# Expert rows by DRAM for two groups and by selection matmuls for two, with gate/up in interleaved halves

## The chip, the cores and the metric

The kernel runs on one core of one Trainium2 chip. The metric is the device time of one execution in microseconds; of several runs the median stands.

## The reference, cut to what matters

A backbone of two layers works on 512 latent tokens and, in the first layer, 256 context tokens, 1024 wide, in float32. Each layer has a mixer and then a hierarchical mixture of experts: a token picks one of four groups, then two of the group's eight experts.

```python
g_idx = jnp.argmax(g_logit, axis=-1)
top_v, top_i = lax.top_k(e_logit, TOP_K)
w = g_prob * jax.nn.softmax(top_v, axis=-1)
e_idx = g_idx[:, None] * EXPERTS_PER_GROUP + top_i
...
(jax.nn.silu(xblk @ w_gate[e]) * (xblk @ w_up[e])) @ w_down[e]
```

Each token's two results, times their weights, are added, gated per channel and added to the stream. An expert's weights are 1024 x 512 twice and 512 x 1024: 6 MiB, of which a layer has 32.

## The kernel before

The whole is one program: mixer 0 (phase_a), experts 0, mixer 1 (phase_c), experts 1 (moe, called once per layer, with 768 and 512 tokens). The stream is kept turned, channels on partitions, in eight tiles XT. Only the parts in moe are changed, and the banks in setup and ps.

Experts are taken in 16 pairs (pr_); the layout has pair r hold two experts of group r % 4. A pair has 128 slots, at most, and usually, 64 for each expert; spare slots of one may go to the other. gather (L1210) is an indirect load on POOL that brings a pair's 128 rows from DRAM (h2d) into xg; a slot with no token fetches row 0, which holds zeros. xpose (L1322) turns them with eight PE transposes. gate_up (L1345) runs 8 steps of two matmuls, the two halves of 64 columns of the array, on the 64 rows of one expert; ACT's silu and two DVE operations make h, turned (L1360) turns it, down (L1369) multiplies by the third weight, and place (L1379) adds both halves to y in SBUF.

When more than 64 rows fall to one expert of a pair, its second half is done in overflow (L1513), under tc.If; if the pair holds more than 128, what is left is gathered into xs and done in blocks of 64 in a second If (a spill). Every engine branches there. HINTED (L45) gives PE, DVE and ACT a hint of the branch ahead of it.

All pairs but the last are "direct": scatter (L1429) writes y to two rows per token in DRAM (yd) by an indirect store on POOL, slots with no token being out of bounds. The last pair's y is split into two float32r parts and added by selection matmuls (combine, L1387, and token_rstd, L1460). At the end fetch_rows (L1553) reads all of yd back by SP, DVE adds a token's two rows, and fetched (L1453) turns them in PE into the banks in which the selection of pair 15 is then accumulated; add_gated adds to XT, squares are summed for the next norm.

Weights come through a ring of eight tiles of 2 MiB, seven of a pool and one extra (spare), in a written order: per pair four gate/up halves, then two downs. load(k) (L971) issues the next k on SP. The tile that a load replaces is the one eight loads earlier, so SP waits for it to be read. What sets the order is the program: PE's order is pinned as written, DVE, ACT and POOL may be ordered within a stretch between two Ifs. Per pair:

```python
if pr_: load(1)
h = gate_up(W[0], ...); h = gate_up(W[1], ..., turn(0, h))
overflow(pr_, W, xts[pr_], y, ys, direct)
load(4)
pd = down(W[0], ht[0], turn(1, h)); load(1)
xts[pr_ + 1] = xpose(...); gather(pr_ + 2)
place(y, 0, pd); place(y, 1, down(W[1], ht[1]))
if direct: scatter(y, yrow[:, pr_:pr_ + 1])
```

PSUM is eight banks: seven in a pool for all uses (ps) and one (bank) that takes every eighth, or, in the expert loop, the gate/up of each pair's first expert.

## Time and profile before

| | |
|---|---|
| Median of 3 runs | 1804.42 us (1800.4 to 1805.56) |
| The profiled execution | 1808.97 us |
| Its span in the trace | 1807.2 us |
| Mean granted clock of TensorE, share of full | 0.944 |
| Busy: PE, PEld, DVE, ACT, POOL | 1533.7, 816.8, 706.2, 410.3, 283.9 us |
| Moved by DMA | 545.23 MB, 302 GB/s over the span |

Slices are 45.2 us. PE is TensorE's matmuls, PEld its weight loads beside them, SPq and POOLq the queues from which DMAs are issued. Busy PE counts waiting inside a pipeline, so 85% does not say that PE is the limit; which wait ends last has to be looked for in each stage. A tile named ring is a weight tile (or a piece of scratch that uses its slot), mk and hb are small tiles of the expert stage, ps and psg are banks.

### The profile page before, as it was taken

Reading aid. Unit: us, or ns where it says so; the run is one execution under the profiler, and the core shown is the slowest. Engines: PE = TensorE matmul, PEld = TensorE weight load, DVE = VectorE, ACT = ScalarE, POOL = GpSimd, SP = SyncE. Lnnn points to the kernel's source line nnn. Section 1 sums busy time; section 2 is a strip of 40 time slices with the busy share of each in tenths; the row PEclk is TensorE's granted clock in tenths of the full one; section 3 lists DMA queues with packets and bytes.
Section 4 is the critical chain, followed back from the end, with each engine's and each line's share of the span. In section 5 each row is a group of like instructions: output and inputs, shape, how many; then the busy total and the mean of one; then the engine's idle time right before and its main releaser. Section 6 shows DMA issues by size and latency. Waiting matters only on the chain. (4 is left out here: it accounts for less than half of the span.)

```text
span 1807.2 us, 21981 instructions
## 1 busy us (share of the span) xinstructions
PE 1533.7 (85%) x8285; PEld 816.8 (45%) x8285; DVE 706.2 (39%) x1342; ACT 410.3 (23%) x930; POOL 283.9 (16%) x232
## 2 busy tenths in 40 slices
PE   6997997988788779767898899996897888888776
PEld 4775686332222223223686878784222322223223
DVE  6799867211111101113636876554111211112115
ACT  4211632110100001001445554332110111011012
POOL 1231343001010101000232202022000101101001
PEclk9999998999989989998999999997899998999998
DMA  8997173799999968999221131488989999999991
GB/s 300 316 298 272 51 291 129 315 399 423 409 426 429 427 247 354 429 427 416 97 88 53 54 104 46 141 293 334 396 343 425 426 385 426 426 387 426 428 366 69
DMA packets 90052, 545.23 MB, mean 302 GB/s; under 512 B 10136, under 2 KB 32296, under 8 KB 63792
## 3 DMA queue, kind: packets, MB, share of 16 engines
q1 hardware_dynamic: 80240, 510.55, 70.7%
q0 software_dynamic: 9536, 31.50, 4.5%
q8 instruction: 112, 1.84, 0.4%
q14 instruction: 164, 1.34, 0.2%
HBM read 511.82 MB, written 34.09 MB: 302 GB/s over the span
## 5 line engine op out<-in xcount | busy, mean ns | idle before, releaser
L56 PE MATMUL ps<-ring,mk 128*64 128x512 f32 x1408 | 326.7, 607 | 35.3 <-DMA ring<-gu 27.2
L56 PE MATMUL ps<-ring,hb 128*64 128x512 f32 x1024 | 265.8, 654 | 100.4 <-DVEq L1517 67.0
L56 PE MATMUL psg<-ring,mk 128*64 128x512 f32 x1024 | 235.8, 610 | 24.2 <-DMA ring<-gu 24.2
L1383 DVE TENSOR_TENSOR mk<-ps,mk 64x512 f32<-64x512 f32 x128 | 88.2, 689 | 319.3 <-PE ps L56 299.5
L56 PEld LDWEIGHTS ps<-ring,mk 128*64 128x64 f32 x1408 | 98.1, 139 | 231.0 <-issue 178.8
L56 PEld LDWEIGHTS ps<-ring,hb 128*64 128x64 f32 x1024 | 72.0, 146 | 239.9 <-issue 160.7
L56 PEld LDWEIGHTS psg<-ring,mk 128*64 128x64 f32 x1024 | 77.6, 140 | 175.6 <-issue 173.0
L1357 DVE SCALAR_TENSOR_TENSOR hb<-mk,mk,ps 128x128 f32<-128x128 f32 x80 | 24.2, 345 | 307.5 <-ACT mk L1353 307.5
L510 DVE SCALAR_TENSOR_TENSOR cv<-u,convw,cv 128x798 f32<-128x798 f32 x120 | 139.1, 1215 | 3.5 <-ACT cv L508 3.0
L1357 DVE SCALAR_TENSOR_TENSOR hb<-mk,mk,psg 128x128 f32<-128x128 f32 x64 | 19.4, 345 | 220.5 <-ACT mk L1353 220.5
L1366 ACT ACTIVATE hb<-ps 128x128 f32<-128x128 f32 x128 | 28.9, 275 | 301.5 <-PE ps L56 301.5
L1211 POOL DMA_INDIRECT xg<-h2d,mk x30 | 30.9, 1029 | 391.3 <-PE ps L56 391.3
L1353 ACT ACTIVATE mk<-psg 128x256 f32<-128x256 f32 x32 | 12.3, 383 | 345.2 <-PE psg L56 188.6
L1567 POOL MEMSET mk<- 128x1024 f32 x32 | 30.5, 953 | 307.3 <-DMA yd<-mk,mk 301.2
L111 PE MATMUL ps<-hh,hi 128*128 128x512 f32 (+1 forms) x232 | 71.4, 365 | 7.2 <-ACT hh L285 7.2
L95 POOL TENSOR_TENSOR lo<-wc,hi 128x1024 fp32r<-128x1024 f32 (+3 forms) x25 | 44.0, 1764 | 175.4 <-ACT hi L89 127.4
L113 PE MATMUL ps<-hl,hi 128*128 128x512 f32 (+1 forms) x232 | 68.6, 349 | 0.0
L115 PE MATMUL ps<-hh,lo 128*128 128x512 f32 (+1 forms) x232 | 68.0, 347 | 0.0
L95 POOL TENSOR_TENSOR lo<-wo,hi 128x512 fp32r<-128x512 f32 x32 | 44.6, 1399 | 114.5 <-ACT hi L89 112.9
L1430 POOL DMA_INDIRECT yd<-mk,mk x30 | 30.2, 1007 | 183.5 <-DVE mk L1383 183.5
L111 PE MATMUL ps<-hi,hi 128*128 128x512 f32 (+1 forms) x191 | 57.1, 348 | 2.2 <-DVE ptl L691 2.0
L113 PE MATMUL ps<-lo,hi 128*128 128x512 f32 (+1 forms) x191 | 55.2, 336 | 3.4 <-POOL lo L95 3.4
(372 smaller groups left out, 2328.8 us busy)
## 6 DMA issues: line engine op xcount, KB each, us to landing
ring<-gu SPq DMA_DIRECT2D x125, 2048.0 KB, 24.0
ring<-dn SPq DMA_DIRECT2D x59, 2048.0 KB, 26.8
mw<-modw SPq DMA_DIRECT2D x72, 512.0 KB, 5.7
yd<-mk SPq DMA_DIRECT2D x20, 512.0 KB, 7.6
ring<-yd SPq DMA_DIRECT2D x10, 1024.0 KB, 12.7
mw<-modh SPq DMA_DIRECT2D x16, 512.0 KB, 7.4
ring<-dn SPq DMA_DIRECT2D x8, 1024.0 KB, 23.0
wi<-w_in SPq DMA_DIRECT2D x12, 512.0 KB, 7.8
```

The source lines that it names most:

```text
L56: i = f(*a, **k)
L95: nc.gpsimd.tensor_tensor(lo, src, hi, op=ALU.subtract)
L111: T.matmul(o, lh, rh, start=start, stop=False)
L113: T.matmul(o, lh, rl, start=False, stop=False)
L115: T.matmul(o, ll, rh, start=False, stop=stop)
L510: nc.vector.scalar_tensor_tensor(acc, u[:, j:j + LO], cw[:, j:j + 1], acc, op0=ALU.mult, op1=ALU.add)
L1211: return G.indirect_dma_start(out=xg, out_offset=None, in_=h2d, in_offset=bass.IndirectOffsetOnAxis(ap=idi[:, pr_:pr_ + 1], axis=0), bound ...
L1357: V.scalar_tensor_tensor(h[b], sg[:, cs_], wcol, po[:, 256 + P * b:384 + P * b], op0=ALU.mult, op1=ALU.mult)
L1366: S.activation(ht[b], po[:, :P], AF.Copy)
L1383: V.tensor_tensor(d, p, d, op=ALU.add)
L1430: G.indirect_dma_start(out=yd, out_offset=bass.IndirectOffsetOnAxis(ap=rows, axis=0), in_=y, in_offset=None, bounds_check=2 * n - 1, oob_i ...
L1567: G.memset(y, 0.0)
```

## The change

The pairs are taken in a new order (ORDER); p is the position, r_ the pair. Pairs of groups 0 and 1 (r_ % 4 < 2) are direct and scattered to yd. Pairs of groups 2 and 3 are split and kept, and combine adds them by selection matmuls during the next pair, in two halves; the last four positions are all of this kind, the last one's combine stands in token_rstd. The last direct pair is at position 11. From position 12 the extra ring tile is the stage: read_back fetches a tile of 128 tokens from yd by two indirect loads on POOL, zeros first, only rows of groups 0 and 1; merge adds a token's two rows, turns them in PE and adds them to XT, two tiles at each position from 13 on.

Gate/up is split: the second half of a pair's first expert runs at the start of its position (the first half in the position before), the second expert's in pieces, between which turning, combine, the first down, the If, and the next pair's transposes stand. The order of loads follows. Slots with no token are now out of bounds in the gather, which then leaves what was there. The hint of the branch is given for PE alone. Banks are six and two.

```diff
-HINTED = [mybir.EngineType.PE, mybir.EngineType.DVE, mybir.EngineType.Activation]
+ORDER = (0, 2, 1, 3, 4, 6, 5, 8, 7, 9, 12, 13, 10, 11, 14, 15)
...
-if self.whole and not hold and self.turn % 8 == 0:
+if self.whole and not hold and self.turn % 4 == 0:
...
-self.psum = E(tc.tile_pool(name="psum", bufs=7, space=PSUM))
-self.psg = E(tc.tile_pool(name="psg", bufs=1, space=PSUM))
+self.psum = E(tc.tile_pool(name="psum", bufs=6, space=PSUM))
+self.psg = E(tc.tile_pool(name="psg", bufs=2, space=PSUM))
...
-    lq, spare = [], []
+    lq, spare, taken = [], [], []
...
+        gu = lambda p, i, h: A["gu"][l, 2 * ORDER[p] + i, h]
+        dn = lambda p, i: A["dn"][l, 2 * ORDER[p] + i]
+        todo = [gu(0, 0, 0)]
+        for p in range(16):
+            todo += [gu(p, 0, 1), gu(p, 1, 0), dn(p, 0), gu(p, 1, 1), dn(p, 1)] + ([gu(p + 1, 0, 0)] if p < 15 else [])
+        for src in todo:
+            a = slot() if len(lq) % 8 != 6 or taken else spare[0].tile([P, 4096], F32, name=self.nm("ring"), tag="ring")
+            for c in ((slice(0, 2048), slice(2048, 4096)) if len(lq) >= 3 * NE - 3 else (slice(0, 4096),)):
+                pin(eng[0].dma_start(out=a[:, c], in_=src[:, c]))
+            lq.append(a)
+            yield
...
+    pad = sm(16)
+    V.tensor_scalar(pad, idf, 0.5, 8192.0, op0=ALU.is_lt, op1=ALU.mult)
+    V.tensor_tensor(idi, pad, idf, op=ALU.add)
...
+    back, bf = keep([2, nt], I32), [sm(nt), sm(nt)]
+    V.tensor_tensor(bf[0], og[:, :, 0], og[:, :, 1], op=ALU.add)
+    V.tensor_scalar(bf[0], bf[0], -8192.0, 8191.0, op0=ALU.mult, op1=ALU.add)
+    V.tensor_tensor(bf[1], self.cols[:, C_TOK:C_TOK + nt], self.cols[:, C_TKL:C_TKL + nt], op=ALU.add)
+    V.tensor_tensor(bf[0], bf[0], bf[1], op=ALU.add)
+    V.tensor_copy(back[:, 0], bf[0])
+    V.tensor_scalar(back[:, 1], bf[0], float(n), None, op0=ALU.add)
...
-    V.tensor_copy(nbf[:, 2:4, 16:32], nbf[:, 2:4, 0:16])
+    for p, r_ in enumerate(ORDER):
+        G.tensor_copy(nbf[:, 2:4, 16 + p:17 + p], nbf[:, 2:4, r_:r_ + 1])
...
+    def weights(p):
+        return [(lambda h, i=i: lq[6 * p + 2 * i + h * (1 + i)].rearrange("p (k c f) -> p k c f", k=4, c=2),
+                 lambda i=i: lq[6 * p + 3 + 2 * i].rearrange("p (k d) -> p k d", k=4)) for i in range(2)]
...
+    def gate_up(po, W, xt, s, ks):
+        for k in ks:
...
+                T.matmul(po[64 * c:64 * c + 64, :], xt[:, k, s], W[0](k // 4)[:, k % 4, c, :], start=k == 0, stop=k == KD - 1)
+    def gated(po, wcol):
+        h = hb[:, 0]
+        S.activation(h.rearrange("p b c -> p (b c)"), po[:, :256], AF.Silu)
...
+    def extra(W, xt, s, wcol):
+        po = self.ps()
+        gate_up(po, W, xt, s, range(KD))
+        return down(W, turned(gated(po, wcol)))
...
-        yh, yl, sel = pend
-        ahead = fetched(0)
...
+            combine([m], *pend)
...
+    def overflow(pos_, pr_, Ws, xt, y, ys, direct):
         shared[0] = {}
-        if pr_ % 8 == 0:
-            spills[:] = nc.values_load_multi_w_load_instructions(nbi[0:1, 2, pr_:pr_ + 8])[1]
-        with tc.If(spills[pr_ % 8] > 0, label=f"ov{l}_{pr_}"):
-            tc.mark_branch_hint_location(f"sp{l}_{pr_}", "LikelyTaken", HINTED)
+        if pos_ % 8 == 0:
+            spills[:] = nc.values_load_multi_w_load_instructions(nbi[0:1, 2, 16 + pos_:24 + pos_])[1]
+        with tc.If(spills[pos_ % 8] > 0, label=f"ov{l}_{pr_}"):
+            tc.mark_branch_hint_location(f"sp{l}_{pr_}", "LikelyTaken", [mybir.EngineType.PE])
...
+    def read_back(t_):
+        v = stage[0][:, 2048 * (t_ % 2):2048 * (t_ % 2) + 2048].rearrange("p (q c) -> p q c", q=2)
+        for q in range(2):
+            G.memset(v[:, q], 0.0)
+            G.indirect_dma_start(
+                out=v[:, q], out_offset=None, in_=yd,
+                in_offset=bass.IndirectOffsetOnAxis(ap=back[:, q, t_:t_ + 1], axis=0),
+                bounds_check=2 * n - 1, oob_is_err=False)
+    def merge(t_):
+        v = stage[0][:, 2048 * (t_ % 2):2048 * (t_ % 2) + 2048].rearrange("p (q c) -> p q c", q=2)
+        V.tensor_tensor(v[:, 0], v[:, 0], v[:, 1], op=ALU.add)
+        for hh in range(2):
+            po = self.ps()
+            for q in range(4):
+                T.transpose(po[:, P * q:P * q + P], v[:, 0, P * (4 * hh + q):P * (4 * hh + q) + P], self.ident)
+            for q in range(4):
+                k = 4 * hh + q
+                x = self.XT[k][:, P * t_:P * t_ + P]
+                V.scalar_tensor_tensor(x, po[:, P * q:P * q + P], gate[:, k, vt(t_):vt(t_) + 1], x, op0=ALU.mult, op1=ALU.add)
+        if t_ + 2 < nt:
+            read_back(t_ + 2)
+    mc = lambda m: slice(P * m, P * m + P)
+    xt = xpose(xg, slice(0, P), "xt", 2)
+    gather(ORDER[1])
     load(1)
...
+    pend, stage = None, []
+    pa = self.bank()
+    gate_up(pa, weights(0)[0], xt, half(0), range(4))
+    slot_weights()
+    for p, r_ in enumerate(ORDER):
+        direct = r_ % 4 < 2
+        y = keep([D], tag="y3", bufs=3)
+        ys = [xs] if direct else [keep([D], F32R, tag="y3", bufs=3) for _ in range(2)]
+        G.memset(y[64:128], 0.0)
+        W = weights(p)
+        tc.mark_branch_hint_location(f"ov{l}_{r_}", "LikelyTaken", [mybir.EngineType.PE])
+        if p == 12:
+            stage.append(spare[0].tile([P, 4096], F32, name=self.nm("ring"), tag="ring"))
+            for t_ in range(2):
+                read_back(t_)
+        gate_up(pa, W[0], xt, half(0), range(4, KD))
+        h = gated(pa, wd[:, 0, 2 * r_:2 * r_ + 1])
+        if p > 12 and 2 * (p - 13) < nt:
+            merge(2 * (p - 13))
+        other = self.bank()
+        gate_up(other, W[1], xt, half(1), range(2))
+        ht = turned(h)
+        if p == 0:
+            spill_table()
+        if pend:
+            combine(range(4), *pend)
+        gate_up(other, W[1], xt, half(1), range(2, 4))
+        if pend:
+            combine(range(4, KD), *pend)
+        place(y, 0, down(W[0], ht), False)
+        overflow(p, r_, W, xt, y, ys, direct)
+        load(4)
+        if p == 15 and not last:
+            early = []
+            for q in range(2):
+                a = slot()
+                for j in range(2):
+                    pin(nc.sync.dma_start(out=a[:, 2048 * j:2048 * j + 2048].rearrange("p (k n) -> p k n", k=2), in_=A["modw"][1, 2, 2 * q + j]))
+                early += [a[:, D * k:D * k + D] for k in range(4)]
+        gate_up(other, W[1], xt, half(1), range(4, 6))
+        own = xt
+        if p < 15:
+            xt = xpose(xg, slice(0, P), "xt", 2)
+            if p < 14:
+                gather(ORDER[p + 2])
+        gate_up(other, W[1], own, half(1), range(6, KD))
+        if p == 11:
+            taken.append(1)
+        else:
+            load(1)
+        h = gated(other, wd[:, 1, 2 * r_ + 1:2 * r_ + 2])
+        if p > 12 and 2 * (p - 13) + 1 < nt:
+            merge(2 * (p - 13) + 1)
+        if p < 15:
+            pa = self.bank()
+            nw = weights(p + 1)[0]
+            gate_up(pa, nw, xt, half(0), range(2))
+        ht = turned(h)
+        if p < 15:
+            gate_up(pa, nw, xt, half(0), range(2, 4))
+        place(y, 1, down(W[1], ht))
+        load(1)
+        if direct:
+            scatter(y, yrow[:, r_:r_ + 1])
+            pend = None
+            continue
+        yh, yl = ys
         for q in range(2):
...
+            cs_ = slice(512 * q, 512 * q + 512)
+            S.activation(yh[:, cs_], y[:, cs_], AF.Copy)
+            V.tensor_tensor(yl[:, cs_], y[:, cs_], yh[:, cs_], op=ALU.subtract)
+        sel = keep([n], F32R, tag="S")
+        V.tensor_scalar(sel, self.cst[:, K_IOTA:K_IOTA + n], idf[:, r_:r_ + 1], None, op0=ALU.is_equal)
+        pend = ((lambda m, a=yh: a[:, mc(m)]), (lambda m, a=yl: a[:, mc(m)]), (lambda m, a=sel: a))
```

## Rows read from the trace of the kernel before

**Rows 1.** Page, part 2: GB/s moved in each of 40 equal slices.
```profile
GB/s 300 316 298 272 51 291 129 315 399 423 409 426 429 427 247 354 429 427 416 97 88 53 54 104 46 141 293 334 396 343 425 426 385 426 426 387 426 428 366 69
```

**Rows 2.** Windows of layer 0: busy us by engine, PEclk, DMA share, GB/s.
```profile
460.00:470.00 10.00, 7.68 (x29) 2.10 (x30) 0.00 (x0) 1.60 (x5) 0.00 (x0) 0.83 0.91 349
660.00:670.00 10.00, 7.88 (x39) 2.94 (x35) 1.03 (x3) 2.49 (x6) 0.17 (x1) 1.00 0.13 54
670.00:680.00 10.00, 8.90 (x40) 2.97 (x42) 0.61 (x2) 0.92 (x3) 0.77 (x1) 1.00 0.08 17
```

**Rows 3.** Windows of layer 1, the same columns.
```profile
1326.00:1338.00 12.00, 10.33 (x47) 2.97 (x42) 0.60 (x2) 0.94 (x3) 0.00 (x0) 1.00 0.46 194
1338.00:1350.00 12.00, 10.60 (x54) 3.88 (x54) 4.12 (x8) 3.13 (x8) 1.03 (x1) 1.00 0.89 350
1458.00:1470.00 12.00, 8.27 (x38) 2.61 (x36) 0.61 (x2) 2.12 (x5) 0.00 (x0) 0.99 0.78 304
1590.00:1602.00 12.00, 7.77 (x36) 2.23 (x32) 0.61 (x2) 2.12 (x5) 0.00 (x0) 1.00 0.74 283
```

**Rows 4.** Timeline of PE, layer 0, pair 1: start, us, what, [idle before].
```profile
343.44 7.04 PE L56 MATMUL psg<-ring,mk 128*64 128x512 f32 x32
...
353.84 0.44 PE L56 MATMUL ps<-cst,hb 128*128 128x128 f32 x2
...
359.29 1.94 PE L56 MATMUL ps<-ring,hb 128*64 128x512 f32 x8 [1.43 <-DVEq L1517]
...
363.40 1.09 PE L56 MATMUL ps<-cst,xg 128*128 128x128 f32 x8
364.42 3.65 PE L56 MATMUL ps<-ring,hb 128*64 128x512 f32 x16
367.90 7.04 PE L56 MATMUL psg<-ring,mk 128*64 128x512 f32 x32
```

**Rows 5.** Timelines of PE and DVE at the ends of layers 0 and 1.
```profile
842.05 5.37 PE L56 MATMUL ps<-ring,hb 128*64 128x512 f32 x24
...
860.83 0.94 PE L56 MATMUL ps<-mk,mk 128*128 128x512 f32 x4
861.62 1.50 PE L56 MATMUL ps<-cst,ring 128*128 128x128 f32 x12
...
849.48 1.29 DVE L1613 TENSOR_TENSOR mk<-mk,mk 128x512 fp32r<-128x512 f32 x2 [0.16 <-issue]
...
871.89 2.19 DVE L295 SCALAR_TENSOR_TENSOR xt<-ps,mod,xt 128x512 f32<-128x512 f32 x4 [0.90 <-PE ps L56]
...
1788.97 1.41 DVE L295 SCALAR_TENSOR_TENSOR xt<-ps,mod,xt 128x512 f32<-128x512 f32 x2 [0.61 <-PE ps L56]
```

**Rows 6.** Timeline of PE, layer 0, pair 2, which overflows.
```profile
384.89 7.09 PE L56 MATMUL ps<-ring,mk 128*64 128x512 f32 x32 [0.75 <-ACT mk L1353]
...
399.70 1.94 PE L56 MATMUL ps<-ring,hb 128*64 128x512 f32 x8 [2.40 <-PEq L1524]
```

**Rows 7.** Timelines of PE, POOL and SP, layer 0, pair 10, which spills.
```profile
652.20 1.08 PE L56 MATMUL ps<-cst,xs 64*128 64x64 f32 x8 [5.20 <-DMA xs<-h2d,mk]
...
683.82 1.94 PE L56 MATMUL ps<-ring,hb 128*64 128x512 f32 x8 [1.40 <-ACTq L1544]
...
641.71 0.96 POOL L1397 DMA_INDIRECT xs<-h2d,mk  x1 [1.43 <-issue]
...
684.05 1.90 SPq L965 DMA_DIRECT2D ring<-dn  x2
```

**Rows 8.** Timeline of POOL, layer 0: a pair's scatter.
```profile
370.28 1.01 POOL L1430 DMA_INDIRECT yd<-mk,mk  x1 [4.49 <-DVE mk L1383]
```

**Rows 9.** Waits: engine, line, waited for: us in total, times, longest.
```profile
POOL mk L1567 <- DMA yd<-mk,mk: 301.2, 28, 11.9
...
PE ps L56 <- DVEq L1517: 67.0, 20, 6.9
```

**Rows 10.** Timeline of DVE, layer 0, pair 15, behind its If.
```profile
838.11 0.62 DVE L1615 TENSOR_SCALAR mk<-cst,mk 128x768 fp32r<-128x768 f32 x1 [5.11 <-DVEq L1517]
```

More of the change, by code (lines that the diff above doesn't have):

```diff
@@ L1214, in gather @@
                     bounds_check=n, oob_is_err=False)
-            gather(0)
+            gather(ORDER[0])
             if nv == 1:
@@ L1362, in turned @@
+            def turned(h):
                 for b in range(2):
                     po = self.ps()
-                    T.transpose(po[:, :P], h[b], self.ident)
-                    ht.append(keep([P], tag=f"ot{b}") if tag == "o" else hb[:, P * (2 + 2 * int(tag) + b):P * (3 + 2 * int(tag) + b)])
-                    S.activation(ht[b], po[:, :P], AF.Copy)
-                return ht
-            def down(W, ht, mid=None):
+                    T.transpose(po[:, :P], h[:, b], self.ident)
+                    S.activation(hb[:, 1, b], po[:, :P], AF.Copy)
+                return [hb[:, 1, b] for b in range(2)]
@@ L1407, in spill_block @@
                 xt = xpose(xs, half(i), "xto", 1)
-                pd = down(W, turned(gate_up(W, xt, slice(0, 64), wc, tag="o"), "o"))
+                pd = extra(W, xt, slice(0, 64), wc)
                 return [(slice(512 * dh, 512 * dh + 512), pd[64 * dh:64 * dh + 64, :]) for dh in range(2)]
@@ L1451, in spill_rest @@
                         spill_combine(half(e % 2), so, *ys)
-            def fetched(m):
-                pss_ = [self.ps() for _ in segs]
-                for t_ in range(nt):
-                    o = P * t_ - segs[vt(t_)][0]
-                    T.matmul(pss_[vt(t_)][:, o:o + P], fy[t_][:, P * m:P * m + P], self.ident, start=o == 0, stop=False)
-                return pss_
             def token_rstd():
@@ L1521, in overflow @@
                         with tc.If(value(1, e, None) > 0):
-                            h = gate_up(Ws[i], xt, half(1 - i), wd[:, 1 - i, e:e + 1], tag="o")
-                            place(y, 1 - i, down(Ws[i], turned(h, "o")), False)
+                            place(y, 1 - i, extra(Ws[i], xt, half(1 - i), wd[:, 1 - i, e:e + 1]), i == 1)
                     with tc.If(value(3, pr_, None) > 0, label=f"sp{l}_{pr_}"):
@@ L1563, in moe @@
-            for pr_ in range(16):
-                direct = pr_ < 15
-                y = keep([D], tag="y3", bufs=2)
-                ys = [xs] if direct else [keep([D], F32R, tag="y3", bufs=2), keep([D], F32R, tag="xg")]
-                G.memset(y, 0.0)
-                if pr_:
-                    load(1)
-                W = [weights(2 * pr_ + i) for i in range(2)]
-                wcol = lambda i: wd[:, i, 2 * pr_ + i:2 * pr_ + i + 1]
-                ht = [None] * 2
-                def turn(i, h, also=None):
-                    def run():
-                        ht[i] = turned(h, str(i))
-                        if also:
-                            also()
-                    return run
-                h = gate_up(W[0], xts[pr_], half(0), wcol(0), None if pr_ else slot_weights, self.bank)
-                tc.mark_branch_hint_location(f"ov{l}_{pr_}", "LikelyTaken", HINTED)
-                h = gate_up(W[1], xts[pr_], half(1), wcol(1), turn(0, h, None if pr_ else spill_table))
-                if not direct:
-                    for j in range(2):
-                        fetch_rows(j)
-                overflow(pr_, W, xts[pr_], y, ys, direct)
-                load(4)
-                if not direct:
-                    if nt > 4:
-                        fetch_rows(2)
-                    if not last:
-                        early = []
-                        for q in range(2):
-                            a = slot()
-                            for j in range(2):
-                                pin(nc.sync.dma_start(out=a[:, 2048 * j:2048 * j + 2048].rearrange("p (k n) -> p k n", k=2), in_=A["modw"][1, 2, 2 * q + j]))
-                            early += [a[:, D * k:D * k + D] for k in range(4)]
-                pd = down(W[0], ht[0], turn(1, h))
-                load(1)
-                if pr_ + 1 < 16:
-                    xts[pr_ + 1] = xpose(xg, slice(0, P), "xt", 2)
-                    if pr_ + 2 < 16:
-                        gather(pr_ + 2)
-                place(y, 0, pd)
-                place(y, 1, down(W[1], ht[1]))
-                if direct:
-                    scatter(y, yrow[:, pr_:pr_ + 1])
```

66 lines of the change are left out of this document (7 added, 59 removed).

## The prediction

> **What bounds it now.** I read the page's slices first [rows 1]: in both expert stages (slices 8 to 19 and 27 to 39) the GB/s line stands at 425 to 429, and elsewhere it is ragged. That plateau is the limit: a pair of experts is six tiles of 2 MiB, 4.9 us each at 427 GB/s, 29.5 us, and about 1 us each for its gather and scatter. Then the windows at finer grain [rows 2, 3]: the plateau breaks only where a pair overflows. The missing GB/s over 427, as time: in layer 0 1.8 us at each of two overflows (one of them is shown) and about 23 at the one spill (18.3 in the two windows, and on past 684); in layer 1 16 over four pairs, in the four windows. The reason is in the code: the ring holds eight tiles, and four are freed only behind the pair's If. Third, the PE timeline of a pair that waits for no data [rows 4]: pitch 24.5 us from the start of one psg row to the next (343.44 to 367.90). The last 0.1 to 0.2 us of a row lies beside the next one, so of the 7.04 of a gate/up 6.9 count, 3.5 of a down's 3.65, 0.36 for turning an expert, 1.0 for eight transposes, and an idle 1.43 at the If. So PE has 6 to 7 us of slack in a pair. Last the tails [rows 5]: in layer 0 PE is through with the last down at 847.4, but the last add into the stream ends on DVE at 874.1, after fetching, adding and turning rows from DRAM.
>
> **The change, part by part.** The sum is made against the profiled execution (1808.97 us, 1.8 beyond its span); the median of the runs is 4.5 us lower, and what I find as a difference is put on the median.
>
> Bytes. Of the DRAM writes and the read back half goes (two groups of four), and the gathers skip their pads: 2048 slots for 1536 rows in layer 0, for 1024 in layer 1. At 4 KB a row and 427 GB/s: in layer 0 about 4.3 us of gathers and 3.7 of scatters by position 11; in layer 1 10 together. This counts only while DMA is the limit. Of the moved read back the half that stays (3.1 and 2.1 MB) now lies ahead of the last weights.
>
> Queues. SP still frees and loads at the same points (four tiles behind the If, one, one), and loses the six and four read-back issues to POOL; the early loads of the next vectors come last there as before. None of this costs, as SP only waits for slots.
>
> Selection matmuls. A step of four matmuls takes 0.79 us in layer 0 (860.83 to 861.62 [rows 5]), eight steps 6.3 us of PE per non-direct pair, seven pairs more; in layer 1, where a step has only the two of 512 columns, two thirds of the work, some 4.5. They lie beside the loads where PE has slack, on the path where a pair overflows. DVE's adds (1.10 a step in layer 0, 0.70 in layer 1 [rows 5]) trail PE by 2.3 us at the end of a combine, since the banks let PE run ahead.
>
> Positions 0 to 11. From one freeing of slots to the next PE needs, where position 1 overflows: rest of position 0 11.7 (half a gate/up, transposes, half of the next one, 0.36, a down), way to the If 10.7 (three quarter steps of 1.72 with the first double, 0.36, 3.5), overflow 14.8 [rows 6]: 37.2, against 31 for six tiles and the side traffic: 6 us dry. At position 4 a combine (6.3) and an overflow meet: 100.7 against 93 since position 1, 8 us dry. So 14 in layer 0 where 3.6 were. In layer 1 only position 1 is short, 7 us, where 16 were, as its third overflowing pair is moved to position 12.
>
> Layer 0, position 12 is pair 10, the spill. At present DMA starts again at 684.05 [rows 7]; five tiles on is tile 72 (the first of position 12): 684 + 25.5 = 709.6; less the spill's 23, less 8 of bytes, plus 10 of new gaps: 689. PE ends position 11 some 7 us later, 696 (half a gate/up, 0.36, a down). Then POOL is what counts. Its queue has the scatter of position 11, 2.2 us after PE's down (368.07 to 370.28) and 1.0 long [rows 4, 8], then two tiles' read back: four memsets (done ahead, if there is time), and four indirect loads that wait for that scatter to land, 11 us as POOL waits today, 301.2 in 28 [rows 9]; then the spill's gather, today 10.5 us from issue to PE's start on it (641.71 to 652.20 [rows 7]). That is 3 + 11.6 + 5 + 1.5 + 10.5 = 32 us after 696, while PE stands at the If 11 us after 696. From there the spill took 31.6 us (652.20 to 683.82); now it also splits (2.7) and combines eight steps (8): the If ends near 696 + 74 = 770. The ring has seven slots from position 12 on, as one is the stage, so DMA runs dry at about 725: 45 us against 23. Queued behind POOL's waits are the gather for position 14, not urgent, and this spill.
>
> Layer 0, from 770 to the end. 17 tiles are left, 84 us of DMA, but PE needs more: rest of position 12 14 (11.7 and 2.3 for DVE's late adds); positions 13 and 14 each 18.1 to the If (a half 3.4, a merge's eight transposes 1.0, quarters and turning 3.8, combine 6.3, down 3.5), the If, 12.8 behind it; position 15 18.1, the If, 3.4, 1.0, gating and turning with nothing beside it 1.7, down 3.5. A merge's add and eight small updates on DVE I cost at nothing, as the rows landed a position earlier; if the cover goes see the second rival.
>
> The If. PE's idle there is 67.0 us in 20 [rows 9], 1.43 where it is short [rows 4]. ACT and DVE lose their hint, so the price isn't shown; below, 1.4; above, 6.1 (DVE's 5.11 [rows 10], and the 1 us by which DVE came to it after PE). I take 4.7: ACT reaches the If 1.3 us after the down, needs 5.1, and PE has 1.7 of matmuls that need no bank; the row of 5.11 is the nearest, since it is a non-direct pair as all of the last four positions are. Sum 14 + 2 x 35.6 + 32.5 = 118: last down ends at 888. The Trainium skill (Runtime: NRT & Kernel Launch, Instruction fetch mechanics) says that a taken branch out of the fetched window stalls for a fetch, which here would speak against dropping hints; no run here shows a branch of ACT or DVE without one. By the rule the sum stays as it is, 1814; by the short row it is 1797.
>
> Tail of layer 0: place and split 3.4 (847.35 to 850.77 [rows 5]), a step's matmuls 0.8, DVE 8 x 1.10: 13.0 instead of 26.7. End of the adds 901 instead of 874.1: **27 later**. What follows is the same chain.
>
> Layer 1. DMA stood until 1602 [rows 3]; tile 72 at 1602 + 25.5 = 1627.5, less 10 of bytes and 9 of gaps: 1608.5. Position 12 overflows: its extra waits for tile 76 (20 us on), 14.8 more: If ends at 1643.5, 3 us dry. PE from there: 11.7; position 13 16.2 + 4.7 + 12.8; position 14 16.2 + 14.8 + 12.8; position 15 15.2 + 4.7 + 8.6: 118, so 1762; DMA, dry again by 14 at position 14, has tile 95 at 1750, ahead of its use. Tail 3.4 + 0.6 + 8 x 0.70 = 10: 1772 instead of 1790.4 [rows 5]: **18 earlier**.
>
> Router, the 16 small copies on POOL, memsets and bank counts (6 and 2 for 7 and 1, so phases before the experts have the same eight): nothing, hidden behind the first gate/up or equal; uncovered, 1 to 3 us a layer. Sum + 9: 1818 for a profiled run, **1814** on the median.
>
> **Rivals.** (a) The spill's gather isn't held on POOL and the Ifs stay short: less 15 (of the 20 that PE stands at the spill, 5 remain as today) and less 16.5 (five untaken Ifs behind 770 and 1643, three and two, at 1.4 for 4.7), **1782**. For: POOL's scatter waits sit today ahead of gathers too, and the spill cost only 5.2 of waiting [rows 7]; many Ifs are short. Against: four indirect loads stand ahead of the gather in program order. (b) The merges aren't covered: the add stands behind the gating on DVE, so each holds PE for the silu, gating and add, 2.5 us, ten merges: **1839**. It decides if the adds are ordered behind the gating. (c) DMA stays the limit to the end (PE finds its slack in the last four positions): each layer ends 17 us or less behind its last tile, 30 earlier: **1744**. Against: 118 us of PE work for 84 of loads. (d) The gaps at positions 1 and 4 of layer 0 don't appear, since PE catches up before each: less 14, 1800, no change. Against: PE's 37.2 there stand against 31.
>
> **How the numbers follow.** 0.3% (5.4 us) is what a measurement can tell. Forecast 0.50, its own range 1797 to 1828: 0.27 slower, 0.18 the same, 0.05 faster. (a) 0.18: faster. (b) 0.20: slower. (c) 0.04: faster. (d) 0.08: the same. So faster 0.27, same 0.26, slower 0.47. The range goes from 1778 to 1839: it leaves out (c), part of (a) and the upper half of (b).
>
> **What would show it.** Right: in layer 0 DMA at nearly nothing for some 45 us at position 12, PE idle there on the spill's rows for about 20, then PE without data waits to the end; the tails' turning of fetched rows gone, 13 us instead of 27; in layer 1 the end 118 us after the If of position 12. Wrong: the spill's gather issued within a few us of the If (a); PE waiting for DVE in the merges (b); PE waiting for ring tiles in positions 13 to 15 (c). A longer or shorter stage before the first expert would also break the sum, as I give it nothing.

## The result, and the profile after

The changed kernel took 1867.99 us (median of four runs, 1867.12 to 1868.48), the kernel before 1804.99 beside it: a ratio of 1.035, interval 1.0329 to 1.0373. That is **63 us slower**; the forecast was 9 slower, and the upper end of its range 1839. The direction was that of the likeliest case, the size was not.

Three boundaries cut the two profiled executions (spans 1807.2 and 1866.7): the first gate/up of a layer's experts, and the end of the last add into the stream. The columns of the rows are start, duration, instruction, count and the idle time before it with what ended it.

```profile
315.78 4.30 PE L56 MATMUL psg<-ring,mk 128*64 128x512 f32 x16
...
906.11 8.50 DVE L295 SCALAR_TENSOR_TENSOR xt<-ps,mod,xt 128x512 f32<-128x512 f32 x16
...
1282.05 2.44 PE L56 MATMUL psg<-ring,mk 128*64 128x512 f32 x8
...
1844.32 5.36 DVE L295 SCALAR_TENSOR_TENSOR xt<-ps,mod,xt 128x512 f32<-128x512 f32 x8
```

| stretch, us | before | after | change | forecast |
|---|---|---|---|---|
| layer 0, first gate/up to last add | 557.8 | 598.8 | +41.0 | +27 |
| from there to layer 1's first gate/up | 375.5 | 367.4 | -8.1 | 0 |
| layer 1, first gate/up to last add | 540.8 | 567.6 | +26.8 | -18 |

So most of the miss, 45 us, lies in layer 1. The windows of the changed kernel (length, busy time of each engine, clock, DMA share, GB/s last) show where the loads stood, to be read against [rows 2, 3]:

```profile
360.00:370.00 10.00, 8.98 (x43) 3.13 (x40) 0.61 (x2) 0.94 (x3) 0.00 (x0) 1.00 0.75 317
370.00:380.00 10.00, 8.25 (x42) 3.03 (x40) 3.29 (x6) 1.43 (x4) 1.03 (x1) 1.00 0.73 272
460.00:470.00 10.00, 8.98 (x44) 2.93 (x42) 0.61 (x2) 1.47 (x4) 0.00 (x0) 1.00 0.77 327
470.00:480.00 10.00, 7.76 (x41) 2.77 (x37) 1.30 (x3) 2.16 (x4) 1.00 (x1) 1.00 0.51 179
720.00:740.00 20.00, 0.42 (x4) 0.46 (x5) 4.18 (x4) 0.00 (x0) 9.87 (x11) 0.58 0.30 91
740.00:760.00 20.00, 16.48 (x71) 5.92 (x71) 2.83 (x6) 2.89 (x7) 1.31 (x2) 0.84 0.06 15
760.00:780.00 20.00, 16.65 (x69) 8.03 (x68) 6.11 (x12) 2.12 (x5) 0.00 (x0) 0.89 0.00 1
780.00:790.00 10.00, 6.69 (x26) 3.58 (x27) 5.86 (x11) 0.60 (x1) 1.00 (x1) 0.74 0.68 253
1334.00:1346.00 12.00, 9.23 (x46) 3.40 (x44) 3.82 (x9) 2.44 (x7) 1.02 (x1) 1.00 0.28 84
1466.00:1478.00 12.00, 10.34 (x44) 3.18 (x40) 1.20 (x3) 0.94 (x3) 0.00 (x0) 0.94 0.06 23
1690.00:1710.00 20.00, 12.78 (x46) 3.97 (x42) 4.43 (x6) 0.94 (x3) 6.08 (x7) 0.82 0.34 106
```

What is missing of 427 GB/s, as time: in layer 0 6.2 us at position 1 and 8.1 at position 4, 59 at the spill; in layer 1 9.6 at position 1, 11.4 at position 5 and 15 at position 12.

Layer 0's spill is where to look first. DVE's queue on the way into the If of position 12, and POOL's beside it:

```profile
707.42 0.60 DVE L1367 SCALAR_TENSOR_TENSOR hb<-hb,mk,psg 128x128 f32<-128x128 f32 x2 [2.43 <-ACT hb L1365]
728.65 2.36 DVE L1555 TENSOR_TENSOR ring<-ring 128x1024 f32<-128x1024 f32 x2 [20.62 <-issue]
732.32 1.84 DVE L1414 TENSOR_SCALAR mk<-cst,mk 64x768 fp32r<-64x768 f32 x2 [1.31 <-DVEq L1518]
```

```profile
717.08 1.02 POOL L1548 DMA_INDIRECT ring<-yd,mk  x1 [10.29 <-DMA yd<-mk,mk]
...
729.93 0.95 POOL L1547 MEMSET ring<- 128x1024 f32 x1 [7.94 <-DVE ring L1555]
731.15 0.99 POOL L1548 DMA_INDIRECT ring<-yd,mk  x1 [0.27 <-POOL ring L1547]
...
735.52 0.94 POOL L1408 DMA_INDIRECT xs<-h2d,mk  x1 [1.14 <-issue]
```

L1555 is the merge's add. In the program it belongs to position 13; the scheduler that lays out each engine's queue has put the first two ahead of the If of position 12 (L1414, the first work inside that If's body, comes after them). So an instruction can cross an If in its engine's queue; the section on the kernel before, which keeps the freedom of order within a stretch between two Ifs, is wrong there. The two wait 20.6 us for rows that POOL could only ask for once the last scatter had landed; and the next read back, which waits for them, now stands ahead of the spill's own gather. The adds of later tiles wait too: in layer 0's position 14 one stands ahead of the gating and waits 16.0 us for its rows, and PE then waits 8.9 for that gating. The Trainium skill (PSUM — Partial Sum Buffer, Engine vs sequencer instructions) says that the queues of VectorE, ScalarE and GpSimd are strictly first in, first out; these rows agree, as nothing behind the adds passed them, not even the branch.

In layer 1's position 12 the same adds stand inside the path of an overflow that PE is already in (PE's rows, then DVE's):

```profile
1688.56 7.09 PE L56 MATMUL ps<-ring,mk 128*64 128x512 f32 x32 [0.81 <-PEq L1518]
1699.94 0.73 PE L56 MATMUL ps<-cst,hb 128*128 128x128 f32 x2 [4.30 <-DVE hb L1367]
1714.60 1.94 PE L56 MATMUL ps<-cst,xg 128*128 128x128 f32 x8 [7.42 <-DVEq L1520]
```

```profile
1696.40 2.53 DVE L1555 TENSOR_TENSOR ring<-ring 128x1024 f32<-128x1024 f32 x2 [17.92 <-DMA ring<-yd,mk]
1699.54 0.60 DVE L1367 SCALAR_TENSOR_TENSOR hb<-hb,mk,ps 128x128 f32<-128x128 f32 x2 [0.61 <-ACT hb L1365]
1707.23 1.39 DVE L1394 TENSOR_TENSOR mk<-ps,mk 64x512 f32<-64x512 f32 x2 [7.09 <-PE ps L56]
1714.81 0.49 DVE L1643 TENSOR_SCALAR mk<-cst,mk 128x512 fp32r<-128x512 f32 x1 [6.18 <-DVEq L1520]
```

There is a second thing in the last rows: DVE is through with its work at 1708.6 and yet takes 6.2 us to get past the inner If (L1520), and PE waits for it. The groups of waits of PE (total, times, longest) show how the branches stand as a whole:

```profile
PE ps L56 <- DVE hb L1367: 26.8, 12, 8.9
PE ps L56 <- DMA xs<-h2d,mk: 20.0, 1, 20.0
PE ps L56 <- DVEq L1520: 20.0, 5, 7.4
PE ps L56 <- ACTq L1514: 16.2, 5, 3.8
...
PE ps L56 <- PEq L1518: 9.9, 5, 4.0
PE ps L56 <- PEq L1514: 9.8, 15, 0.7
```

At the outer If (L1514) PE loses 0.66 most times, and 26 us in 20 waits with those put down to ACT, where [rows 9] had 67.0 in 20 for DVE alone; at the inner ones (L1518 in, L1520 past the spill) it now pays up to 4.0 and 7.4. And of DVE's waits this group alone takes 60 us:

```profile
DVE ring L1555 <- DMA ring<-yd,mk: 60.0, 6, 17.9
```

### The profile page after: what moved, and what is told of

It reads as the page before. It is cut to its first block, busy times and chain, and to the rows that moved or that the text cites. A ratio compares the mean times of both kernels' runs of the same rounds, so it can differ in the third digit from the quotient of the medians.

```text
span 1866.7 us, 23016 instructions
## 1 busy us (share of the span) xinstructions
PE 1613.2 (86%) x8573; PEld 873.5 (47%) x8573; DVE 829.3 (44%) x1612; ACT 460.8 (25%) x1012; POOL 314.9 (17%) x292
## 5 line engine op out<-in xcount | busy, mean ns | idle before, releaser
L56 PE MATMUL psg<-ring,mk 128*64 128x512 f32 x2048 | 509.9, 630 | 48.3 <-DMA ring<-gu 46.9
L56 PEld LDWEIGHTS psg<-ring,mk 128*64 128x64 f32 x2048 | 143.2, 143 | 329.8 <-issue 290.8
L295 DVE SCALAR_TENSOR_TENSOR xt<-ps,mod,xt 128x256 f32<-128x256 f32 (+1 forms) x243 | 142.9, 651 | 52.5 <-PE ps L56 29.2
L1394 DVE TENSOR_TENSOR mk<-ps,mk 64x512 f32<-64x512 f32 x74 | 51.0, 689 | 246.3 <-PE ps L56 214.6
L56 PE MATMUL ps<-mk,mk 128*128 128x512 f32 (+3 forms) x468 | 102.4, 367 | 17.4 <-DVE mk L56 8.1
L1396 ACT ACTIVATE mk<-ps 64x512 f32<-64x512 f32 x66 | 39.0, 592 | 244.4 <-PE ps L56 234.8
L56 PE MATMUL ps<-cst,xg 128*128 128x128 f32 x256 | 43.1, 323 | 54.7 <-DVEq L1520 20.0
L1367 DVE SCALAR_TENSOR_TENSOR hb<-hb,mk,psg 128x128 f32<-128x128 f32 x128 | 38.8, 345 | 111.5 <-ACT hb L1365 111.4
L56 PEld LDWEIGHTS ps<-mk,mk 128*128 128x128 f32 x416 | 70.5, 198 | 32.4 <-DVE xt L295 8.3
L56 PE MATMUL ps<-ring,mk 128*64 128x512 f32 x256 | 63.3, 651 | 10.0 <-PEq L1518 9.9
```

The source lines that it names most:

```text
L56: i = f(*a, **k)
L295: self.nc.vector.scalar_tensor_tensor(x, ps[:, :w], g[:, m, v:v + 1], x, op0=ALU.mult, op1=ALU.add)
L1367: V.scalar_tensor_tensor(h[:, b], h[:, b], wcol, po[:, 256 + P * b:384 + P * b], op0=ALU.mult, op1=ALU.mult)
L1394: V.tensor_tensor(d, p, d, op=ALU.add)
L1396: S.activation(d, p, AF.Copy)
```

## The experiments

Three candidates came out of this: the overflow in the last positions (theory A), the added work itself (B), and, from the profile of the first of these, DVE's adds (C); beside them the branches and the place of the third quarter (D). Two kernels leave rows out of layer 0's stream, and so layer 1's router picks other experts; only their layer 0 is read.

**Where in the stage the loss lies.** First the order of the pairs:

```diff
-ORDER = (0, 2, 1, 3, 4, 6, 5, 8, 7, 9, 12, 13, 10, 11, 14, 15)
+ORDER = (0, 2, 1, 14, 4, 6, 5, 8, 10, 9, 12, 13, 7, 11, 3, 15)
```

> The changed kernel with pairs 10 and 14 moved from positions 12 and 14 to 8 and 3, and 7 and 3 in their places, so that no pair that overflows lies in the last four positions of either layer. Theory A: most of the loss is made where an overflow meets the read back, its merge and a ring of seven; then the spill's rows come without POOL's wait for the read back (20 us of PE become some 5), no inner branch and no late merge holds PE in the last positions, and it takes 1810 to 1830. Theory B: the loss is the added work itself (selection matmuls, interleave, quarters), wherever an overflow stands; then 1850 to 1870.

Measured 1860.32 (ratio 1.0307, 1.0279 to 1.0335): only 8 us less, so theory A falls. The number lies in B's range, but the profile names another cause. The If of position 12 isn't taken there in either layer, and still PE stands at it for 30 us (PE's row, then DVE's):

```profile
792.39 1.94 PE L56 MATMUL ps<-cst,xg 128*128 128x128 f32 x8 [30.33 <-DVEq L1514]
```

```profile
778.54 1.22 DVE L1555 TENSOR_TENSOR ring<-ring 128x1024 f32<-128x1024 f32 x1 [25.97 <-issue]
789.30 1.22 DVE L1555 TENSOR_TENSOR ring<-ring 128x1024 f32<-128x1024 f32 x1 [9.53 <-DMA ring<-yd,mk]
792.42 0.74 DVE L1643 TENSOR_SCALAR mk<-cst,mk 128x768 fp32r<-128x768 f32 x1 [1.90 <-DVEq L1514]
```

In layer 1 it is 31.18. In the order of the change this wait lay under the spill and the overflow; moving those away uncovered it. Next, without the read back and the merge:

```diff
-                if p == 12:
-                    stage.append(spare[0].tile([P, 4096], F32, name=self.nm("ring"), tag="ring"))
-                    for t_ in range(2):
-                        read_back(t_)
...
-                if p > 12 and 2 * (p - 13) < nt:
-                    merge(2 * (p - 13))
...
-                if p == 11:
-                    taken.append(1)
-                else:
-                    load(1)
+                load(1)
```

> The changed kernel without the read back and the merge: the rows of the direct pairs are never added into the stream (this part of the computation is left out), and the ring keeps its eighth slot to the end. Theory A: POOL's four loads are no longer ahead of the spill's gather, DVE's adds no longer wait for landings, 8 us of transposes and the dry time of a ring of seven go: 1825 to 1840. Theory B (selection matmuls and branches are the loss): only the transposes go, 1855 to 1865.

Measured 1812.17 (1.0036, 1.0018 to 1.0055), 56 less; layer 0 took 568.8 instead of 598.8. All that hangs on the read back is thus worth 30 us in layer 0, far more than its transposes. Without the selection matmuls (both calls of `combine` in the loop dropped):

> The changed kernel without the selection matmuls of all pairs but the last (their rows are never added into the stream; the split and the selection matrix are still made). If seven times 6.3 and 4.5 us of PE were on the path: 1868 less 76, 1792. By my steps they are on it in positions 13 to 15 of each layer (19 and 13.5 us) and at an overflow or two: 1825 to 1840. If DVE's adds hold the last positions anyway: 1850 to 1865.

Measured 1838.84 (1.0198, 1.0179 to 1.0217), layer 0 584.8: 14 us there, where my steps put 19 or more. The total lies in the range that my steps gave. The selection matmuls are on the path no more than forecast; theory B is a part, and it was in the sum.

**The adds taken off DVE.** First with identity matmuls that turn both halves into one bank:

```diff
-                V.tensor_tensor(v[:, 0], v[:, 0], v[:, 1], op=ALU.add)
...
-                        T.transpose(po[:, P * q:P * q + P], v[:, 0, P * (4 * hh + q):P * (4 * hh + q) + P], self.ident)
+                        for z in range(2):
+                            T.matmul(po[:, P * q:P * q + P], v[:, z, P * (4 * hh + q):P * (4 * hh + q) + P], self.ident, start=z == 0, stop=z == 1)
```

> The changed kernel with the merge's add taken from DVE: PE turns both halves of a row with a matmul by the identity into the same bank, 48 more small matmuls in layer 0 and 32 in layer 1. In the changed kernel DVE's adds of the first two tiles stand ahead of the If of position 12 in its queue, and wait there for rows that land some 30 us later. Theory C: these adds are the largest part of the loss, as they keep DVE, and with it every If, gating and release of slots, waiting; in this order of pairs a part lies under the spill of layer 0, so 1830 to 1845 against 1868. Theory B (the work itself): the matmuls cost 1 us a tile more, 1865 to 1880.

Measured 1848.19 (1.0259, 1.0235 to 1.0284), 20 less, between the two ranges. The same in the other order:

> The last edit together with the order of e2_order (no overflow in the last four positions). In e2_order PE stood 30.3 and 31.2 us at the If of position 12, which is not taken there. Theory C: both go, 1795 to 1815 against its 1860. Theory B: 1855 to 1870.

Measured 1828.04 (1.0142, 1.0125 to 1.0159), 32 less than e2_order; the 61 us of waiting at the If are gone, but the total is above C's range, and the matmuls of ten tiles take 38.4 us (e5_pe_merge) where the transposes took 10.9. With the hints of before as well:

> The last one with the hints for PE, DVE and ACT. If the hints are worth what e1_hints gained (19 us) in any order: 1780 to 1795. If they gained there only at the two inner Ifs of the last positions (7.4 to 1.75 us each), no more than 5 below e6_pe_merge_order.

Measured 1824.72 (1.0126, 1.0102 to 1.015), 3 less. Then with transposes, each half added to the stream by itself:

```diff
-                V.tensor_tensor(v[:, 0], v[:, 0], v[:, 1], op=ALU.add)
-                for hh in range(2):
+                for z, hh in ((0, 0), (1, 0), (0, 1), (1, 1)):
...
-                        T.transpose(po[:, P * q:P * q + P], v[:, 0, P * (4 * hh + q):P * (4 * hh + q) + P], self.ident)
+                        T.transpose(po[:, P * q:P * q + P], v[:, z, P * (4 * hh + q):P * (4 * hh + q) + P], self.ident)
```

> Another way to take the merge's add off DVE's queue ahead of the Ifs, in the order of the change: both halves of a row are turned by transposes and added to the stream one after the other (per tile 8 more transposes, about 1.1 us, and 8 more updates of 0.27 us, for an add of 1.2 us). Theory C: as e5_pe_merge (1848), less what its identity matmuls cost more than transposes (3.84 against 2.2 us a tile, ten tiles): 1830 to 1840. If the adds were not the cause and e5_pe_merge gained in another way: 1850 or more.

Measured **1818.39** (1.0074, 1.0049 to 1.0098): 50 us less than the changed kernel, more than expected, though PE has ten times eight transposes more. PE's waits in it:

```profile
PE ps L56 <- DMA xs<-h2d,mk: 13.2, 1, 13.2
...
PE ps L56 <- DVEq L1520: 8.8, 5, 1.8
PE ps L56 <- DVE hb L1367: 8.3, 9, 1.0
```

The wait on the spill's rows fell by 6.8 us, since no second read back stands ahead of the gather, and the waits on DVE's gating from 26.8 to 8.3. But the inner If fell too, from 20.0 to 8.8, and nothing was done to it: part of the 50 is not the adds'. With order and hints:

> The same with the order of e2_order and the three hints. e7_pe_merge_order_hints took 1825; less 1.7 us on ten tiles, 1808. What is left over 1803 is then PE's own work in the last four positions (118 us by my steps for 84 of loads) and the dry times at the overflows: 1803 to 1813. If PE were not the bound there: 1820 to 1828.

Measured 1807.55 (1.002, 1.0003 to 1.0037), as theory C said. Whether the adds' place in the queue is all, was tried by holding them on DVE behind the gating:

```diff
-            def merge(t_):
+            def merge(t_, h):
+                one = keep([1], tag="cur")
+                V.tensor_scalar(one, h[:, 0, 0:1], 0.0, 1.0, op0=ALU.mult, op1=ALU.add)
...
-                V.tensor_tensor(v[:, 0], v[:, 0], v[:, 1], op=ALU.add)
+                V.scalar_tensor_tensor(v[:, 0], v[:, 1], one, v[:, 0], op0=ALU.mult, op1=ALU.add)
```

> The changed kernel with the same adds on DVE, made to need a value of the gating ahead of them in the program, so that they can't stand ahead of an If in DVE's queue. If their place in the queue is the cause: as e10_two_turns (1818), plus up to 1.4 us by which each of ten merges now holds PE behind gating and add, less the 1.1 us a tile that e10's transposes cost: 1815 to 1830. If the engine or the work is the cause (the adds wait for the landing wherever they stand): 1850 to 1868.

Measured 1874.45 (1.0399, 1.0386 to 1.0413): no gain at all, and above both ranges, so theory C as I had put it falls too. The spill's wait did fall to 13.1 and no add waits for a landing any more, but now every merge holds PE behind silu, gating and add:

```profile
PE ps L56 <- DVE ring L1557: 26.4, 10, 2.8
PE ps L56 <- DVEq L1520: 19.8, 5, 7.4
```

That is 2.6 us of waiting on each of ten merges, the wait that rival (b) named, but not the whole price. The matmuls behind such a wait are slower for a while. Here are, behind the wait of 2.66 us that ended at 836.7, PE's quarter of a gate/up and the window it lies in (columns as above):

```profile
837.74 3.56 PE L56 MATMUL psg<-ring,mk 128*64 128x512 f32 x8
```

```profile
836.70:841.50 4.80, 4.78 (x19) 1.89 (x19) 2.16 (x8) 0.00 (x0) 3.89 (x4) 0.64 1.01 434
```

The granted clock is 0.64 there, so part of the window ran at 1.2 GHz and the rest at 2.4; with the clock at 1.00 the same quarter takes 1.94. Over ten merges this adds some 14 us, so that a merge costs about 4 us and ten about 40 (an estimate from these rows). An add on DVE between the landing and PE's transposes thus costs much the same in both places: ahead of the If it waits for rows, behind it PE waits for the add. What helps is to have none there. (The inner If stands at 19.8 here, as in the changed kernel.)

**The branches.** All hints back on the changed kernel (`[mybir.EngineType.PE]` replaced by `HINTED` in both places):

> The changed kernel with both branch hints given to PE, DVE and ACT again, as before the change. If the dropped hints are what the late branches cost (7.4 us at an inner If of layer 1, 3.4 to 3.9 at some outer ones), it comes down by 15 to 30 us from 1868, to 1838 to 1853. If the hints were never worth their place (before the change, with them, PE stood 67.0 us in 20 waits at the outer If), it goes up or stays: 1865 to 1890. My theory puts no more than 10 us on them: 1858 to 1868.

Measured 1849.0 (1.0257, 1.0225 to 1.029), 19 less, where my theory allowed no more than 10. To tell the inner If from the outer one, and from the adds, only its hint was given back, on two kernels:

```diff
-                    tc.mark_branch_hint_location(f"sp{l}_{pr_}", "LikelyTaken", [mybir.EngineType.PE])
+                    tc.mark_branch_hint_location(f"sp{l}_{pr_}", "LikelyTaken", HINTED)
```

> The changed kernel with the hint at the inner If for PE, DVE and ACT, at the outer If still for PE alone. If DVE's missing hint makes the 7.4 us waits at the inner If, they become 1.75 (11 us in layer 1) and it takes 1850 to 1858, nearly all of what e1_hints gained (19). If the outer hints made e1_hints faster: 1864 to 1870.

> The same hint on e10_two_turns (1818), where PE's waits at the inner If are 1.75 in each of five already. If the hint only takes away the stalls: 1814 to 1821, no change. If it is worth something beyond them: 1800 to 1812.

Measured 1855.71 (1.0296, 1.0271 to 1.0321) and 1817.33 (1.008, 1.0055 to 1.0105): 12 us on the one, nothing on the other, both as expected. PE's waits in e16_inner_hints, and then in e17_two_turns_inner_hints (lines are one further down: L1368 is the gating, L1519 the way into the body of an overflow, L1521 the inner If past the spill):

```profile
PE ps L57 <- DVE hb L1368: 23.1, 12, 7.4
...
PE ps L57 <- PEq L1519: 9.6, 5, 4.8
...
PE ps L57 <- DVEq L1521: 8.8, 5, 1.8
```

```profile
PE ps L57 <- DVEq L1521: 8.9, 5, 1.9
PE ps L57 <- DVE hb L1368: 8.3, 9, 1.0
...
PE ps L57 <- PEq L1519: 3.8, 5, 0.8
```

And the overflow of layer 1's position 5, PE's wait on the way into its body and its 32 matmuls, in the same two:

```profile
1462.05 9.82 PE L57 MATMUL ps<-ring,mk 128*64 128x512 f32 x32 [4.78 <-PEq L1519]
```

```profile
1441.00 7.09 PE L57 MATMUL ps<-ring,mk 128*64 128x512 f32 x32 [0.74 <-PEq L1519]
```

The inner If is alike in both, and yet not all of the 38 us between them (1855.71 - 1817.33) are the adds'. In layer 1 8.9 us lie ahead of position 12, where no merge stands (377.4 against 368.5 from the first gate/up to the transposes behind position 11's If). These rows are a part of it: a longer way in, and behind it matmuls at a granted clock of 0.72 (part of the time at 1.2 GHz, the rest at 2.4) where the other has 1.00. It goes with the build (what the queues and the code of one program come out as) and not with the adds: the five ways in take 8.7 us in e5_pe_merge, which has no such add on DVE, and 4.0 in e9_quarter, which has all of them. So the adds are worth **27 to 30 us** (35.6 between the profiled spans, or 38.4 between the medians, less 8.9), and that net of 8.7 us of transposes more. Of the 50, another **12** are stalls of DVE's unhinted branch, and the rest is PE's ways in. On the kernel before (with pads and banks, below) the hints were taken from DVE and ACT:

> The kernel before with the pads, the banks and the hints for PE alone. In the kernel before, PE stood 67.0 us in 20 waits at the outer If, in the changed one mostly 0.66 to 3.9 at an If not taken; DMA hides most of it, the last pair of each layer doesn't (5.1 and 6.1 us). If the hints for DVE and ACT make those waits: 1770 to 1778 against 1783. If it is the order of work that made them shorter: 1780 to 1786.

Measured 1793.66 (0.9944, 0.9932 to 0.9957), 11 slower than with them, which neither range allowed. So dropping these hints was a loss in either kernel; here 8 of the 11 lie in layer 0 (560.2 against 552.1), but which branch they belong to no run settles. PE's waits for DVE at the outer If got no shorter by it (72.1 us in 20, 60.7 with the hints); that PE waits less there in the changed kernel thus comes from something else in the change, and the order of work is the likely part.

**The third quarter.** In PE's queue of the changed kernel the quarter written behind the If stands ahead of it (PE's order, too, is not all as written), so PE reaches the If only with the fifth tile. One matmul by zeros inside the body holds it behind:

```diff
                 with tc.If(spills[pos_ % 8] > 0, label=f"ov{l}_{pr_}"):
                     tc.mark_branch_hint_location(f"sp{l}_{pr_}", "LikelyTaken", [mybir.EngineType.PE])
+                    T.matmul(other[0:64, 0:1], zb[:, 0:64], zb[:, 0:1], start=False, stop=False)
```

> The changed kernel with the third quarter of the second gate/up held behind the If on PE, as it stands in the program (in the changed kernel's queue it stands ahead, so that PE reaches the If only when the fifth tile of the pair has landed): one matmul of a column of zeros into the same bank inside the If's body keeps it there. Theory D: in layer 1 the If of position 5 comes 4.6 us earlier (2.7 of waiting and 1.9 of matmuls), that of position 12 3 us; the dry times of DMA shrink by as much there, and at positions 1 and 4 by 2: 1853 to 1863 against 1868. Rival: what is gained there is lost at the Ifs that are not taken, where the quarter lay beside the wait for the other engines: 1866 to 1880.

> e10_two_turns with the quarter held behind the If as in e9_quarter. If the fifth tile ahead of the If is a cause of its own (dry times at the overflows of layer 1, positions 1 and 5, and layer 0, 1 and 4): 1798 to 1806 against 1818. If e9_quarter gained because DVE's adds moved with it: 1814 to 1822.

Measured 1847.69 (1.024, 1.0216 to 1.0263) and 1810.1 (1.0038, 1.0023 to 1.0053). The first gained more than expected, 20 us, but in its build PE's wait for DVE at the inner If is 9.3 instead of 20.0, and its ways into the bodies take 4.0 instead of 9.9; the second, where neither build has a wait above 1.8 at the inner If, gives the quarter alone: 8 us, between the two ranges (its ways in take 6.9 against 3.7 in e10_two_turns, so 8 is rather low).

**What gained.** On the kernel before, the banks alone, and banks and pads together (these are the change's own lines):

```diff
-        if self.whole and not hold and self.turn % 8 == 0:
+        if self.whole and not hold and self.turn % 4 == 0:
...
-        self.psum = E(tc.tile_pool(name="psum", bufs=7, space=PSUM))
-        self.psg = E(tc.tile_pool(name="psg", bufs=1, space=PSUM))
+        self.psum = E(tc.tile_pool(name="psum", bufs=6, space=PSUM))
+        self.psg = E(tc.tile_pool(name="psg", bufs=2, space=PSUM))
...
-            V.tensor_copy(idi, idf)
+            pad = sm(16)
+            V.tensor_scalar(pad, idf, 0.5, 8192.0, op0=ALU.is_lt, op1=ALU.mult)
+            V.tensor_tensor(idi, pad, idf, op=ALU.add)
```

> The kernel before with the banks split six and two, and nothing else. With the pads as well it took 1783, against 1805. If the banks give the 5.7 us by which the stretch between the expert stages got shorter: 1797 to 1800, and the pads 15. If the banks give nothing: 1803 to 1806, and the pads all 22.

> The kernel before with two small parts of the change alone: the gathers skip their pads, and the PSUM banks are split six and two. If the stretch from layer 0's end to layer 1's first gate/up got 5.7 us shorter because of the banks, and the pads' bytes (512 rows and 1024 rows of 4 KB, 4.9 and 9.8 us at 427 GB/s) count while DMA is the limit, it takes 1785 to 1795 instead of 1805. If neither counts, 1803 to 1807.

Measured 1797.98 (0.9971, 0.9955 to 0.9987) and **1782.6** (0.9882, 0.9847 to 0.9918): the banks give 5, the pads 15, about what their bytes say. This is the fastest kernel of the study. All repairs of the changed kernel together:

> Two turns, the quarter behind the If, the order without overflows in the last four positions, and the three hints. If they add (50, 15, 8 and 3 to 10 us against 1868): 1785 to 1795. If the last four positions are bound by PE's work, as e10_two_turns_order_hints (1808) says, the quarter gives only its part ahead of them: 1795 to 1802. The kernel before with pads and banks, 1783, would stay ahead in both.

Measured 1788.05 (0.9915, 0.9902 to 0.9928): 80 us below the change as it was made and 16 below the kernel before, but behind the two small parts alone.

## Why the prediction was wrong

**The step that failed**: "A merge's add and eight small updates on DVE I cost at nothing, as the rows landed a position earlier". I took the adds to be reached where the program has them, with their rows in place. The first two of each layer stood a position earlier in DVE's queue, ahead of the If and ahead of the landing, and held gating, the If, POOL's next read back and with it the spill's gather; later ones held a gating. That is 27 to 30 us by e16 and e17. Behind the gating they cost no less (e12), so "nothing" was wrong for either place. With the adds off DVE and the quarter where the program puts it (e13) the kernel that my sum described takes 1810.1, against the 1814 forecast; that this is so near is in part luck, as errors below cancel.

**The second one**: the price of the Ifs. The 4.7 that I took at an outer If not taken was 0.66 most times; what I had taken over unseen, within the 14.8 of an overflow, was the inner Ifs (2.40 in [rows 6]), 7.4 us at layer 1's positions 12 and 14. Unhinted DVE was the right suspect at the wrong branch (12 us, e16).

**The third**: "In layer 1 only position 1 is short, 7 us". Positions 1 and 5 were short by 9.6 and 11.4. The rows of position 5 show it: PE gets the fifth tile, does the quarter, and only then comes to the If, where the way in costs 4 us more and the matmuls behind it 2.3 more than the usual 7.09 (position 5 overflows like position 1, and the prediction put its gap at nothing without a reason):

```profile
1456.07 2.63 PE L56 MATMUL psg<-ring,mk 128*64 128x512 f32 x8 [2.70 <-DMA ring<-gu]
1462.68 9.42 PE L56 MATMUL ps<-ring,mk 128*64 128x512 f32 x32 [3.98 <-PEq L1518]
...
1479.11 1.06 PE L56 MATMUL ps<-cst,xg 128*128 128x128 f32 x8 [1.75 <-DVEq L1520]
```

The quarter is not the cause of the long way in: in e10_two_turns it stands ahead as well, and the way in at position 5 is 0.73.

What came as forecast: the dry times, in which DMA had no free slot to load into, of layer 0's positions 1 and 4 (6.2 and 8.1 against 6 and 8), the spill in 46 against 42, the tail of layer 0 (11.5 against 13). PE's wait for the spill's rows came as forecast by luck (20.05 against 20): with the adds away it is 13.2 (e10), since the rows come some 3 us sooner than my 32 behind the last down and PE is at the If after 16 and not 11; the second read back ahead of the gather, which the sum did not have, made up the 7. From the If of position 12 to the last down layer 0 took 117.6 against 118, but by two errors that cancel: shorter outer Ifs, and 10 us of waits on DVE (8.86 and 1.39). The spill's If ended at 785.5 and not at 770: position 11 ended 7 later, as PE had position 12's first tile at 695.8 and not at 689; the gaps were as said, so little of the 8 us put down to bytes came by then. Whether it was the scatters' bytes that didn't pay isn't settled; the gathers' do (15 us on the kernel before). The bank counts, put at nothing, gave 5 us.

Two slips in the sums changed nothing: layer 1's four windows of [rows 3] show three pairs and not four, and rival (c)'s 30 us earlier in each layer make 1754 and not 1744.

Of the rivals, (a) fell at the spill, where the gather was held, and was half right on the Ifs. (b) named the engine and the right wait for the place it named (2.6 us each in e12, 2.5 said), without the slower matmuls behind it; but that was not the place. (c) and (d) didn't occur. The rule of the Trainium skill (Runtime: NRT & Kernel Launch, Instruction fetch mechanics) that a taken branch out of the fetched window stalls for a fetch was set aside in one sentence. At the outer If the trace doesn't bear it out (0.66 without hints, below the short row of 1.4 that would have made the sum 1797); for DVE at the inner one it would fit, 7.4 us against 1.75, but no run shows where the code lay, so the cause of that stall stays open.

## What to carry to other kernels

Ask of every new instruction not where the program has it but where the queue of its engine can have it: one that needs no result of a branch may stand ahead of it, and if it waits for a transfer the branch waits too, and with it all engines and every slot freed behind it. Cost such a wait from issue to landing, not from the program's order; the cure was to leave no add between the landing and PE, not to move it. And measure the small parts of a large change alone: here two of them were worth 22 us and the rest lost 85.

## What the runs showed of the hardware that was not expected

- A branch without a hint on DVE costs PE either 1.75 us or 4.6 to 7.5 at the inner If, and which one differs from build to build at places that no edit touched: none of five was long in e2_order and e10_two_turns, one in e5_pe_merge (5.0) and e6_pe_merge_order (7.46), two in the changed kernel, in e12_add_behind and in e9_quarter (4.55 and 4.78). With the hint none was (e1, e7, e16, e17). A difference of some 10 us between two builds can be this alone.
- PE's way into the body of an overflow, with its hint in every build, took 0.7 to 0.9 us or 2.6 to 5.8: two of five were long in the changed kernel, e1, e2, e12 and e16, one in e5, e6, e7 and e13, none in e9, e10, e14 and e17.
- A wait of 2.6 us on PE cost about 4, as the granted clock behind it was 0.64 for 4.8 us (e12); behind a way in of 4.8 us 32 matmuls took 9.82 at 0.72, where they take 7.09 (e16, e17).
- Turning and adding a block of 128x128 by two f32 matmuls with the identity took 0.48 us (38.4 us for 80 blocks); a transpose of one block 0.136 (10.9 for 80), of two 0.245 (19.6).
- Indices beyond the bound made a gather cheaper by about the bytes of the rows left out: 5.6 us in layer 0 for 512 rows and 8.8 in layer 1 for 1024 (e11 against e4), where 4 KB a row at 427 GB/s says 4.9 and 9.8.
